# The modulation of a transformer block in units of 256 features, and two thirds of them later in the load order

## The chip, the cores and the metric

The kernel runs on one core of a Trainium2 chip. The metric is the device time of one execution in microseconds. PE is TensorE, DVE is VectorE, ACT is ScalarE, POOL is GpSimd and SP is SyncE, whose queue issues the weight loads.

## What is computed

The input is 256 tokens of 1024 features and one condition vector `c`. The first block modulates its layers by the condition, and only this block is touched:

```
cond = silu(c)                                   # 1024
mod  = cond @ ada_w + ada_b                      # 1024 x 6144
sh1, sc1, g1, sh2, sc2, g2 = split(mod, 6)       # 1024 features each
h = rms_norm(x, norm1) * (1 + sc1) + sh1
y = concat(attn_a(h), attn_b(h), gla(h), lru(h)) @ w_out     # each from its columns of h @ w_in
x = x + g1 * y
h = rms_norm(x, norm2) * (1 + sc2) + sh2
x = x + g2 * moe(h)                              # 32 experts, top 4
```

A second block of two layers with dense weights follows; it has no modulation.

## The kernel before

All is kept with features on the partitions. Weights come in units of 1 MB (128 x 2048 f32). `enqueue` lists the units of the first block in a fixed order, and `load` (line 306) issues the next load on SP's queue whenever one of five buffers is free: two of tag rawx, three of tag raw. A buffer is given back by `drop` (line 328), in the order of the program. There are two kinds of units.

A weight unit, of `w_in` (11 of them, the list WIN, line 1703: cqk, cv, cr, aq, ak, av, dx, dg, bq, bk, bv) or of `w_out` (wo1, four of them, in the order lru, attn_b, attn_a, gla), is split into two halves of 128 x 1024, each into a high part (a cast on ACT) and a low part (a subtraction on DVE or POOL). The raw buffer is free when its second low part is made. A product takes three matmuls (high x high, high x low, low x high), so a unit costs 48 matmuls of 256 columns (`unit_mm`, line 610; `vstep`, line 2263).

A modulation unit (`ada`, 24 of them) is used raw, by a function that stands in the queue beside it. In `ada_unit` (line 1758) the stationary operand is one eighth of `cond`, repeated to 32 columns, and the moving operand is the unit. Before, a unit holds 128 input rows of 2048 output features. Its four matmuls of 512 columns go to four strips of 32 partitions of one PSUM bank, and eight units, one per eighth of the input, add up there. After the eighth the bank is copied to SBUF, four transposes turn it and one DVE add with the bias fills 16 columns of `mod` (`ada_turn`, line 1780). Group 0 (units 0 to 7) gives sh1 and sc1, group 1 g1 and sh2, group 2 sc2 and g2. One bank is held from the first unit to the last.

`block1_units` (line 1692) sets the order of the loads: ada 0 to 7, cqk, cv, then each of the nine other weight units of `w_in` with two ada units behind it as far as these last, then the four of wo1.

The order of the instructions on each engine is made when the program is built. A planner (class Clocks, line 43) keeps a modelled clock of each engine and of the DMA. While the matmuls of a projection are written out, `stir` (line 485) steps other work between them: the four branches gla, aa (attn_a), ab (attn_b) and lru are generators, each started when its projections are there. Where a branch must be finished, `rounds` (line 502) steps what is ready first. Both call `pump` (line 356), which also makes the splits ahead and uses modulation units: a unit is used when the planner's clock of PE has come to within 0.5 us of its modelled landing. `use_up` forces all units up to a number. On the chip each engine works through its list in order; a modelled landing that comes later on the chip is a wait of the whole engine.

In `mixer1` (line 2271) the mean square and the eight normed rows z come first. Then `use_up(7)` forces the first eight modulation units, A = (1 + sc1) * norm1 is made in one instruction, and a loop over the eight feature tiles k makes the modulated rows (ACT Identity with scale and bias, two DVE operations for the low part). cqk and cv are split at k = 0 and k = 3, and from k = 3 on their products, and those of the small weight for gla, follow feature by feature. Then come the nine projections. `use_up` of unit 23 stands ahead of the products with wo1; ahead of the last of them (gla's) `settle` finishes all deferred small work. The experts' weights go to tiles of the next phase, in the memory of the mixer's pages.

Of the kernel before, what the change touches and what calls it, by code (L numbers as in the profile page):

```python
# [14 lines left out]
ALU = mybir.AluOpType  # L15
P = 128
T = 256
KD = 8
# [177 lines left out]
class Core:  # L196
    EARLY, SOON, MORE, POOL, ACT, PLAIN, LEAN = 0.7, 0.0, 2.0, 2.0, 1.0, -2.0, 0.5
    static = False
    FINE, LATE = 2, 1.0
    stepping = GIVE = False  # L200
    KEEP = ("raw", "whi", "wlo", "ident", "causal", "ones_d", "ones_g", "eps", "one", "one32", "junk", "id16", "s5_r4", "vecs")
    MID = ("iota", "four", "group", "upper", "ones", "mod", "adaA", "rw", "rb")
    NRAW = 3
# [2 lines left out]
    pages, stop = None, 1 << 30  # L206
# [149 lines left out]
    def pump(self):  # L356

        c = self.nc
        while self.sl < self.sh and c.written(self.halves[self.sl][0]) <= max(c.tensor.clock, min(self.v.clock, self.q.clock)) + self.SOON:
            self.split_low()  # L360
        while self.sh <= min(self.most, 2 * self.last - 1) and self.arrived(self.order[self.sh // 2], c.scalar) and self.free(c.scalar):
            self.split_high()
        for u in sorted(self.uses):
            if not self.arrived(u, c.tensor):
                break
            self.use(u)

# [1312 lines left out]
class Kernel(Block2):  # L1680
    NE, B1, NP42, NP22, NP12, NPAIR = 32, 2.0, 9, 8, 10, 4
    MIX = dict(EARLY=0.2, SOON=-0.5, LEAN=2.0, GIVE=True)
    WAT = 0, 3
    S3 = 0
    DM3 = 6
    DM1, DM2 = 7, 7
# [5 lines left out]
    def block1_units(self):  # L1692
        a = self.a
        ada = [(("ada", u), a["adaw"][u], lambda raw, n, u=u: self.ada_unit(u, raw, n)) for u in range(24)]
        win = [((n, 0), a["win1"][i]) for n, i in self.WIN]
        yield from ada[:8] + win[:2]
        for j, u in enumerate(win[2:]):
            yield u
            yield from ada[8 + 2 * j:10 + 2 * j]
        for g in self.YORD:  # L1700
            yield ("wo1", g), a["wo1"][g]

    WIN = [("cqk", 6), ("cv", 7), ("cr", 8), ("aq", 0), ("ak", 1), ("av", 2), ("dx", 9), ("dg", 10), ("bq", 3), ("bk", 4), ("bv", 5)]
    YORD = (3, 1, 0, 2)
# [47 lines left out]
    def ada_load(self):  # L1752
        c8, self.cond = self.t([P, KD], "c8"), self.t([P, KD, 32], "cond")
        self.nc.scalar.dma_start(c8, self.a["c"])
        self.nc.scalar.activation(self.cond, c8[:, :, None].to_broadcast([P, KD, 32]), AF.Silu)
        self.mod = self.t([P, 48], "mod")

    def ada_unit(self, u, raw, n):

        nc = self.nc  # L1760
        g, k = divmod(u, KD)
        if not u:
            self.adaps = self.bank()
        lab, self.lab = self.lab, "ada"
        for i in range(4):
            nc.tensor.matmul(self.adaps[i * 32:i * 32 + 32], self.cond[:, k], raw[:, i * 512:i * 512 + 512], start=k == 0, stop=k == KD - 1,
                             skip_group_check=True, tile_position=(0, i * 32))
        if k == KD - 1:
            rows = self.t([P, 512], "adarow")
            nc.scalar.copy(rows, self.adaps)  # L1770
            if g == 2:
                self.give(ps=1)
            if g:
                self.defer(lambda: self.ada_turn(g, rows))
            else:
                for _ in self.ada_turn(g, rows):
                    pass
        self.lab = lab

    def ada_turn(self, g, rows):  # L1780

        nc = self.nc
        yield from self.need(ps=1)
        self.lab = "ada"
        ps = self.psum()
        for j in range(4):
            nc.tensor.transpose(ps[:, j * P:(j + 1) * P], rows[:, j * P:(j + 1) * P], self.ident)
        yield
        at = lambda t: t[:, g * 16:g * 16 + 16].rearrange("p (i j) -> p i j", j=4)
        self.v.tensor_tensor(at(self.mod), ps.rearrange("p (j i r) -> p i j r", j=4, r=32)[:, :, :, 0], at(self.vec("adab")), op=ALU.add)  # L1790
        self.give(ps=1)

    def ada_norm(self, x, ms, g, sh, sc, emit):
        v = self.v
# [476 lines left out]
    def mixer1(self, x):  # L2271
        nc, a = self.nc, self.a
        v, q = self.v, self.q
# [13 lines left out]
            sq = self.square(x[:, 2 * i:2 * i + 2].rearrange("p a t -> p (a t)"), sq)  # L2287
        ms = self.mean([sq], self.ones_d)
        z = self.unit_rows(x, ms)
        self.use_up(7)  # L2290
        xn = self.fm(dt=F32R), self.fm(dt=F32R)
        A = self.t([P, KD], "adaA", 2)
        v.scalar_tensor_tensor(A, self.mod[:, 8:16], 1.0, self.vec("norm1"), op0=ALU.add, op1=ALU.mult)
        gps, pss = self.bank()[:16, :T], [self.bank() for _ in range(2)]
        ws, done = [], 0
        for k in range(KD):
            if k in self.WAT:
                j = len(ws) // 2
                self.split_ahead(2 * j + 1, v)
                ws += [self.half((self.WIN[j][0], 0), 2 * j + 1 + i) for i in range(2)]  # L2300
            t, sc, sh = self.p1(), A[:, k:k + 1], self.mod[:, k:k + 1]
            nc.scalar.activation(xn[0][k], z[k], AF.Identity, scale=sc, bias=sh)
            v.tensor_scalar(t, z[k], sc, sh, op0=ALU.mult, op1=ALU.add)
            v.tensor_sub(xn[1][k], t, xn[0][k].bitcast(F32))
            if k == 1:
                self.split(gw, *gwh)
            while k > 2 and done <= k:
                j, done = done, done + 1
                xs = xn[0][j], xn[1][j]
                for m in range(2):  # L2310
                    self.mm3(pss[0][:, m * T:(m + 1) * T], [w[:, j * P:(j + 1) * P] for w in ws[m]], xs, j == 0 and m == 0, j == KD - 1)
                self.vstep(pss[1], ws[2 + j // 4], xs, j)
                self.mm3(gps, (gwh[0][:, j], gwh[1][:, j]), xs, j == 0, j == KD - 1)
        self.split_ahead(self.uh + self.S3)
        y = self.fm(dt=F32R), self.fm(dt=F32R)
# [21 lines left out]
        for j, (n, _) in enumerate(self.WIN):  # L2337
            self.lab = n
            ps = pss[j] if j < 2 else self.bank()
# [30 lines left out]
                    ths[i] = self.spawn(self.attn_a(b[:2], b[2], y) if i == 0 else self.attn_b(b[:2], b[2], y) if i == 1 else  # L2370
                                        self.gla(*b, gl, wg2, rg, y) if i == 2 else self.lru(*b, y))
        acc = None
        self.use_up(self.keys.index(("ada", 23)))
        for g in self.YORD:
            self.finish(ths[g])
            acc = acc or [self.bank() for _ in range(4)]
            self.lab = "wo1"
            first, last = g == self.YORD[0], g == self.YORD[-1]

            def part(i, m, w):  # L2380
                self.mm3(acc[m // 2][:, (m % 2) * T:(m % 2 + 1) * T], [z[:, m * P:(m + 1) * P] for z in w],
                         (y[0][2 * g + i], y[1][2 * g + i]), first and i == 0 and m % 2 == 0, last and i == 1)
            if last:
                self.settle()
                ws = [self.half(("wo1", g), i + 1) for i in range(2)]
                for b in range(4):
                    for i in range(2):
                        for m in (2 * b, 2 * b + 1):
                            part(i, m, ws[i])
                sqs = []  # L2390

                def add(i):
                    v.tensor_add(sqs[i][:, :T], sqs[i][:, :T], sqs[i][:, T:])
                    if i:
                        v.tensor_add(sqs[i][:, :T], sqs[i][:, :T], sqs[i - 1][:, :T])
                for i in range(4):
                    for k in (2 * i, 2 * i + 1):
                        v.scalar_tensor_tensor(x[:, k], acc[i][:, (k % 2) * T:(k % 2 + 1) * T], self.mod[:, 16 + k:17 + k], x[:, k],
                                               op0=ALU.mult, op1=ALU.add)
                    sqs.append(self.p2([P, 512]))  # L2400
                    nc.scalar.activation(sqs[i], x[:, 2 * i:2 * i + 2].rearrange("p a t -> p (a t)"), AF.Square)
                    if i:
                        add(i - 1)
                break
            for i in range(2):
                w = self.half(("wo1", g))
                for m in range(KD):
                    part(i, m, w)
                    if m % self.FINE == self.FINE - 1 and m < KD - 1:
                        self.stir(self.budget)  # L2410
                self.tick(self.budget)
# [534 lines left out]
def host_block1(d, vecs, off):  # L2946
    c = np.ascontiguousarray
    f = lambda n: np.asarray(d[n])[0]
    out = {}
# [4 lines left out]
        vecs.append(v.reshape(-1, P).T)  # L2954
    out["x"] = c(np.asarray(d["x"])[0].T.reshape(8, P, T).transpose(1, 0, 2))
    out["c"] = c(np.asarray(d["c"]).reshape(8, P).T)
    out["adaw"] = c(f("ada_w").reshape(8, P, 3, 2048).transpose(2, 0, 1, 3).reshape(24, P, 2048))
    addv("adab", f("ada_b"))
    addv("norm1", f("norm1_g"))
    addv("norm2", f("norm2_g"))  # L2960
    w = f("w_in")
    sizes = (256, 256, 256, 256, 256, 256, 128, 128, 256, 16, 256, 256, 256)
    p = dict(zip("aq ak av bq bk bv cq ck cv cg cr dx dg".split(), np.split(w, np.cumsum(sizes)[:-1], axis=1)))
# [77 lines left out]
```

## Time and profile before

| | us |
|---|---|
| median of 3 runs | 2945.7 |
| lowest and highest | 2922.97, 2946.81 |
| the profiled execution | 2948.41 |
| its span, first to last instruction | 2946.7 |
| PE busy in it | 2673.1 (91%) |
| DVE, ACT, POOL busy | 1670.8, 1009.0, 423.4 |
| mean granted clock of PE | 0.967 |

The durations in the rows below are of the one profiled execution. Nearly all instructions are recorded by one helper, so they all carry line 172; they are told apart by the names of their tiles, which begin with the part of the program that made them. The units' buffers are called raw and rawx, high and low parts whi and wlo, and the first letters of a buffer's name are those of the part that happened to issue its load. The granted clock is 1.00 at 2.4 GHz and 0.50 at 1.2 GHz; a value between them is a mean over the stretch.

### The profile page before, as it was taken

Reading aid. Unit: us, or ns where it says so; the run is one execution under the profiler, and the core shown is the slowest. Engines: PE = TensorE matmul, PEld = TensorE weight load, DVE = VectorE, ACT = ScalarE, POOL = GpSimd, SP = SyncE. Lnnn points to the kernel's source line nnn. Section 1 sums busy time; section 2 is a strip of 40 time slices with the busy share of each in tenths; the row PEclk is TensorE's granted clock in tenths of the full one; section 3 lists DMA queues with packets and bytes.
Section 4 is the critical chain, followed back from the end, with each engine's and each line's share of the span. In section 5 each row is a group of like instructions: output and inputs, shape, how many; then the busy total and the mean of one; then the engine's idle time right before and its main releaser. Section 6 shows DMA issues by size and latency. Waiting matters only on the chain.

```text
span 2946.7 us, 55258 instructions
## 1 busy us (share of the span) xinstructions
PE 2673.1 (91%) x22931; PEld 2049.9 (70%) x22931; DVE 1670.8 (57%) x2968; ACT 1009.0 (34%) x1474; POOL 423.4 (14%) x386
## 2 busy tenths in 40 slices
PE   6867898988898888988999999889999999998998
PEld 3656333332333333368999999889999999998998
DVE  3485324242333311056679787667575698977755
ACT  3273100001000000033454655434454455654544
POOL 2322100000000000034012131143010100221100
PEclk7788999999999999999999999999999999999999
DMA  8504999999999999977554544377455455553453
GB/s 333 214 31 146 420 420 405 415 420 420 420 415 416 420 419 419 418 243 206 203 184 167 189 172 170 137 160 241 172 189 180 149 180 189 186 190 125 159 185 115
DMA packets 145421, 754.62 MB, mean 256 GB/s; under 512 B 45760, under 2 KB 50320, under 8 KB 58640
## 3 DMA queue, kind: packets, MB, share of 16 engines
q1 hardware_dynamic: 127584, 710.42, 63.2%
q0 software_dynamic: 17440, 40.61, 5.3%
q8 instruction: 185, 3.03, 0.4%
q14 instruction: 68, 0.56, 0.1%
q10 hardware_dynamic: 144, 0.00, 0.0%
HBM read 735.98 MB, written 14.97 MB: 255 GB/s over the span
## 4 chain that ended last, share of the span: by engine, by line
PE 45%; DVE 7%; DMA 2%; ACT 2%; issue 1%; ACTq 0%; DVEq 0%
PE ffn_ps L172 21%; PE x_ps L172 4%; PE bb_ps L172 3%; PE z_ps L172 3%; PE glu_ps L172 3%; PE g_ps L172 3%; PE bnd_ps L172 2%; PE wo_ps L172 2%; DMA ffn_raw<-gu 1%; DVE ffn_wlo L172 1%; PE ssd_ps L172 1%; PE u_ps L172 1%; DVE ffn_p L172 1%; DVE x_p L172 1%; DVE bnd_p L172 1%
## 5 line engine op out<-in xcount | busy, mean ns | idle before, releaser
L172 PE MATMUL ffn_ps<-bnd_p,ffn_whi 128*128 128x256 f32 x2560 | 468.3, 285 | 0.5 <-ACT ffn_whi L172 0.5
L172 DVE TENSOR_TENSOR ffn_wlo<-ffn_raw,ffn_whi 128x1024 fp32r<-128x1024 f32 x232 | 305.5, 1322 | 189.9 <-ACT ffn_whi L172 189.8
L172 PEld LDWEIGHTS ffn_ps<-bnd_p,ffn_whi 128*128 128x128 f32 x2560 | 404.0, 194 | 0.9 <-ACT ffn_whi L172 0.9
L172 PE MATMUL ffn_ps<-bnd_p,ffn_wlo 128*128 128x256 f32 x1280 | 365.7, 286 | 17.5 <-DVE ffn_wlo L172 17.5
L172 ACT CAST ffn_whi<-ffn_raw 128x1024 fp32r<-128x1024 f32 x232 | 240.6, 1046 | 310.8 <-PE ffn_ps L172 242.1
L172 PE MATMUL down_ps<-up_place,tr_p 128*32 128x512 f32 (+1 forms) x2048 | 243.1, 612 | 81.1 <-DMA up_place<-edn 81.1
L172 PE MATMUL ffn_ps<-ffn_p,ffn_whi 128*128 128x256 f32 x1408 | 259.6, 286 | 11.3 <-ACT ffn_whi L172 11.3
L172 PEld LDWEIGHTS ffn_ps<-bnd_p,ffn_wlo 128*128 128x128 f32 x1280 | 248.5, 194 | 19.0 <-DVE ffn_wlo L172 19.0
L172 PE MATMUL up_ps<-down_place,prep_p 128*32 128x512 f32 (+1 forms) x1920 | 224.7, 596 | 21.0 <-DMA down_place<-eup 21.0
L172 PE MATMUL up_ps<-up_place,prep_p 128*32 128x512 f32 (+1 forms) x2048 | 230.5, 595 | 7.5 <-DMA up_place<-eup 7.0
L172 PEld LDWEIGHTS down_ps<-up_place,tr_p 128*32 128x32 f32 x2048 | 68.2, 112 | 243.0 <-issue 202.9
L172 PEld LDWEIGHTS ffn_ps<-ffn_p,ffn_whi 128*128 128x128 f32 x1408 | 223.3, 195 | 11.7 <-ACT ffn_whi L172 11.7
L172 DVE TENSOR_SCALAR glu_p<-up_ps 128x512 f32<-128x512 f32 x64 | 44.2, 691 | 311.2 <-PE up_ps L172 311.2
L172 PE MATMUL ffn_ps<-ffn_p,ffn_wlo 128*128 128x256 f32 x704 | 201.5, 286 | 1.1 <-DVE ffn_wlo L172 1.1
L172 PEld LDWEIGHTS up_ps<-up_place,prep_p 128*32 128x32 f32 x2048 | 61.8, 109 | 149.8 <-issue 129.8
L172 PEld LDWEIGHTS up_ps<-down_place,prep_p 128*32 128x32 f32 x1920 | 57.0, 109 | 130.7 <-issue 127.0
L172 DVE COPY scat_p<-down_ps 128x512 f32<-128x512 f32 x16 | 11.1, 692 | 240.4 <-PE down_ps L172 240.4
L172 PEld LDWEIGHTS ffn_ps<-ffn_p,ffn_wlo 128*128 128x128 f32 x704 | 137.1, 195 | 1.9 <-DVE ffn_wlo L172 1.9
L172 DVE TENSOR_TENSOR ffn_p<-ffn_p,ffn_p 128x256 f32<-128x256 f32 (+1 forms) x184 | 99.6, 547 | 41.6 <-ACT ffn_p L172 41.4
L172 ACT COPY prep_p<-prep_ps 128x512 f32<-128x512 f32 x16 | 9.4, 585 | 291.2 <-PE prep_ps L172 291.2
L172 ACT COPY tr_p<-tr_ps 128x512 f32<-128x512 f32 x32 | 18.7, 585 | 223.6 <-PE tr_ps L172 223.6
L172 PE MATMUL bb_ps<-ssd_p,ba_whi 128*128 128x256 f32 x416 | 84.2, 302 | 9.5 <-ACT ssd_p L172 6.1
(794 smaller groups left out, 5887.4 us busy)
## 6 DMA issues: line engine op xcount, KB each, us to landing
up_place<-eup SPq DMA_DIRECT2D x128, 1024.0 KB, 10.8
up_place<-edn SPq DMA_DIRECT2D x128, 1024.0 KB, 13.7
down_place<-eup SPq DMA_DIRECT2D x120, 1024.0 KB, 14.7
ffn_raw<-gu SPq DMA_DIRECT2D x75, 1024.0 KB, 4.9
ffn_raw<-dn SPq DMA_DIRECT2D x40, 1024.0 KB, 5.0
x_raw<-win SPq DMA_DIRECT2D x22, 1024.0 KB, 5.0
z_raw<-win SPq DMA_DIRECT2D x16, 1024.0 KB, 5.1
g_raw<-win SPq DMA_DIRECT2D x10, 1024.0 KB, 4.9
```

The lines of the kernel that those rows point to most:

```text
L172: return f(out, *args, **kw)
```

## The change

A modulation unit now holds all 1024 input rows of 256 output features, and is complete by itself. The host sorts the features so that unit k of the first eight has features 128k to 128k+127 of sh1 and of sc1; units 8 to 23 take the other 4096 in order. A unit is eight matmuls of 256 columns, two into each strip of 32 partitions; a copy of 128 x 256 on ACT, two small matmuls with a constant matrix `four`, which add up the four strips and turn the result, and one DVE add of two columns. `mixer1` forces unit k only at feature tile k, and makes A there, column by column.

The load order becomes: ada 0, 1, cqk, ada 2, 3, cv, ada 4 to 7, cr, aq, ak, then av, dx, dg, bq, bk and bv with one ada unit behind each (8 to 13), wo1 of lru, ada 14 to 17, wo1 of attn_b, ada 18 to 23, wo1 of attn_a, wo1 of gla. `pump` uses a unit only when the planner's clock of PE is 2 us past its modelled landing, and a PSUM bank and one of two places for modulation units are free. `use_up` of unit 23 moves to just ahead of the last product with wo1.

```diff
@@ Core
+    ADAM, PSADA = 2.0, 0
@@ pump
         for u in sorted(self.uses):
-            if not self.arrived(u, c.tensor):
+            if u not in self.raws or c.written(self.raws[u][0]) > c.tensor.clock - self.ADAM or not self.has(dict(ps=1 + self.PSADA, ada=1)):
                 break
             self.use(u)
@@ Kernel
+    ADA0, ADA1, ADAM = 5, (4, 6, 0, 0), 2.0
@@ block1_units
-        yield from ada[:8] + win[:2]
-        for j, u in enumerate(win[2:]):
+        yield from ada[:2] + win[:1] + ada[2:4] + win[1:2] + ada[4:8]
+        rest = iter(ada[8:])
+        for j, u in list(enumerate(win))[2:]:
             yield u
-            yield from ada[8 + 2 * j:10 + 2 * j]
-        for g in self.YORD:
+            if j >= self.ADA0:
+                yield next(rest)
+        for g, n in zip(self.YORD, self.ADA1):
             yield ("wo1", g), a["wo1"][g]
+            for _ in range(n):
+                yield next(rest)
@@ ada_unit, ada_turn (new)
+        self.grab(ps=1, ada=1)
+        ps, w = self.psum(), raw.rearrange("p (k c) -> p k c", k=KD)
+        for k in range(KD):
+            i = k % 4
+            nc.tensor.matmul(ps[i * 32:i * 32 + 32, :T], self.cond[:, k], w[:, k], start=k < 4, stop=k >= 4, skip_group_check=True,
+                             tile_position=(0, i * 32))
+        if u < 8:
+            for _ in self.ada_turn(u, ps):
+                pass
+        else:
+            self.defer(lambda: self.ada_turn(u, ps), after=ps[:, :T])
...
+        rows = self.t([P, T], "adarow", 2)
+        nc.scalar.copy(rows, ps[:, :T])
         yield
+        for j in range(2):
+            nc.tensor.matmul(ps[:, T + j * 32:T + j * 32 + 32], rows[:, j * P:(j + 1) * P], self.four, start=True, stop=True, skip_group_check=True)
+        yield
+        at = self.ada_at(u)
+        self.v.tensor_tensor(self.mod[:, at], ps[:, T:T + 64].rearrange("p (j r) -> p j r", r=32)[:, :, 0], self.vec("adab")[:, at], op=ALU.add)
+        self.give(ps=1, ada=1)
@@ mixer1
-        self.use_up(7)
...
-        v.scalar_tensor_tensor(A, self.mod[:, 8:16], 1.0, self.vec("norm1"), op0=ALU.add, op1=ALU.mult)
...
+            self.use_up(self.keys.index(("ada", k)))
+            v.scalar_tensor_tensor(A[:, k:k + 1], self.mod[:, 8 + k:9 + k], 1.0, self.vec("norm1")[:, k:k + 1], op0=ALU.add, op1=ALU.mult)
...
-        self.use_up(self.keys.index(("ada", 23)))
         for g in self.YORD:
...
             if last:
+                self.use_up(self.keys.index(("ada", 23)))
                 self.settle()
```

## Rows read from the trace of the kernel before

**Rows 1.** The table by stage: busy us and instructions of each engine, granted clock, DMA.

```profile
core 0: us, PE busy (x) PEld busy (x) DVE busy (x) ACT busy (x) POOL busy (x), PEclk, DMA share, GB/s
...
60.30:136.70 76.40, 61.73 (x372) 45.59 (x368) 33.05 (x57) 19.79 (x31) 22.41 (x14) 0.75 0.66 248
136.70:179.30 42.60, 42.60 (x395) 38.62 (x394) 34.32 (x57) 24.51 (x41) 20.36 (x10) 1.00 0.30 104
179.30:217.90 38.60, 14.82 (x73) 10.51 (x72) 29.15 (x78) 31.25 (x93) 5.52 (x3) 0.74 0.00 1
217.90:249.40 31.50, 28.93 (x221) 27.86 (x222) 15.86 (x31) 12.25 (x23) 12.52 (x5) 0.88 0.00 1
...
290.00:1250.00 960.00, 848.20 (x7418) 317.86 (x7414) 284.52 (x829) 71.69 (x125) 25.60 (x39) 0.99 1.01 417
```

**Rows 2.** The timeline of SP's DMA queue: start us, us, what.

```profile
17.29 3.60 SPq L172 DMA_DIRECT2D mix_raw<-win  x2
...
254.13 23.37 SPq L172 DMA_DIRECT2D moe_place<-eup  x8
```

**Rows 3.** The list of PE's waits, 60.3 to 179.3 us.

```profile
PE mix_ps L172 <- DMA aq_raw<-adaw: 7.7, 2, 4.9
PE mix_ps L172 <- DMA cr_raw<-adaw: 5.1, 4, 1.7
PE gla_ps L172 <- DVE gla_p L172: 1.7, 1, 1.7
```

**Rows 4.** The timeline of PE, three stretches: start us, us, what, [wait].

```profile
14.22 1.03 PE L172 MATMUL mix_ps<-k_raw,k_cond 128*32 128x512 f32 x8
...
81.33 1.07 PE L172 MATMUL mix_ps<-cr_raw,k_cond 128*32 128x512 f32 x8 [1.74 <-DMA cr_raw<-adaw]
...
93.05 1.94 PE L172 MATMUL mix_ps<-aq_raw,k_cond 128*32 128x512 f32 x8 [2.84 <-DMA aq_raw<-adaw]
...
95.72 0.63 PE L172 MATMUL aq_ps<-mix_p,cr_whi 128*128 128x256 f32 x2
96.15 0.41 PE L172 MATMUL aq_ps<-mix_p,cr_wlo 128*128 128x256 f32 x1
...
140.17 0.39 PE L172 MATMUL dx_ps<-mix_p,ak_whi 128*128 128x256 f32 x2
140.40 0.28 PE L172 MATMUL dx_ps<-mix_p,ak_wlo 128*128 128x256 f32 x1
```

**Rows 5.** The same, only gla_ps: PE, PEld, DVE, ACT, clock, DMA share, GB/s.

```profile
60.30:136.70 76.40, 12.64 (x82) 10.62 (x82) 7.36 (x11) 0.00 (x0) 0.75 0.66 248
```

**Rows 6.** The same, only k_cond: PE, PEld, ACT, clock, DMA share, GB/s.

```profile
11.30:28.80 17.50, 11.80 (x64) 1.76 (x64) 0.00 (x0) 0.76 1.02 421
...
60.40:179.40 119.00, 15.57 (x97) 2.18 (x96) 0.00 (x0) 0.84 0.53 196
```

**Rows 7.** The timeline of all engines where the first modulation is finished.

```profile
13.38 2.50 DVE L172 TENSOR_TENSOR mix_p<-k_h,mix_p 128x512 f32<-128x512 f32 x4
...
29.25 2.00 ACT L172 CAST mix_whi<-mix_raw 128x1024 fp32r<-128x1024 f32 x2
...
30.62 0.17 DVE L172 TENSOR_TENSOR k_mod<-ada_ps,k_vecs 128x16 f32<-128x16 f32 x1 [14.73 <-PE ada_ps L172]
...
30.91 2.36 DVE L172 TENSOR_TENSOR mix_wlo<-mix_raw,mix_whi 128x1024 fp32r<-128x1024 f32 x2
...
33.62 1.09 ACT L172 ACTIVATE mix_p<-mix_p,k_mod,mix_adaA 128x256 fp32r<-128x256 f32 x2
...
34.27 1.04 PE L172 MATMUL mix_ps<-mix_p,mix_whi 128*128 128x256 f32 x2 [3.70 <-ACT mix_p L172]
```

**Rows 8.** DMA issues of the first 300 us: count, KB, median us to landing.

```profile
aq_raw<-win SPq DMA_DIRECT2D x3, 1024.0 KB, 4.9
```

**Rows 9.** The timeline of ScalarE, a copy of this size from PSUM.

```profile
232.18 0.37 ACT L172 CAST mix_p<-ab_ps 128x256 fp32r<-128x256 f32 x1 [0.22 <-PE ab_ps L172]
```

**Rows 10.** The timeline of PE, two small matmuls.

```profile
261.29 0.31 PE L172 MATMUL moe_ps<-k_ident,route_p 32*128 32x32 f32 x2 [0.56 <-ACT route_p L172]
```

More of the change, by code (lines that the diff above doesn't have):

```diff
@@ L1756, in ada_load, with ada_at @@
         self.mod = self.t([P, 48], "mod")
+        self.room["ada"] = 2
+    def ada_at(self, u):
+        return slice(u, u + 9, 8) if u < 8 else slice(2 * u, 2 * u + 2)
     def ada_unit(self, u, raw, n):
         nc = self.nc
-        g, k = divmod(u, KD)
-        if not u:
-            self.adaps = self.bank()
+        self.grab(ps=1, ada=1)
         lab, self.lab = self.lab, "ada"
-        for i in range(4):
-            nc.tensor.matmul(self.adaps[i * 32:i * 32 + 32], self.cond[:, k], raw[:, i * 512:i * 512 + 512], start=k == 0, stop=k == KD - 1,
-                             skip_group_check=True, tile_position=(0, i * 32))
@@ L1768, in ada_unit @@
[L1768 to L1777, printed above, removed]
+        ps, w = self.psum(), raw.rearrange("p (k c) -> p k c", k=KD)
[3 more added lines that the diff above has]
+                             tile_position=(0, i * 32))
@@ L1778, in ada_unit, with ada_turn @@
+        if u < 8:
[3 more added lines that the diff above has]
+            self.defer(lambda: self.ada_turn(u, ps), after=ps[:, :T])
         self.lab = lab
-    def ada_turn(self, g, rows):
+    def ada_turn(self, u, ps):
         nc = self.nc
[L1783 to L1787, printed above, removed]
-        yield
-        at = lambda t: t[:, g * 16:g * 16 + 16].rearrange("p (i j) -> p i j", j=4)
-        self.v.tensor_tensor(at(self.mod), ps.rearrange("p (j i r) -> p i j r", j=4, r=32)[:, :, :, 0], at(self.vec("adab")), op=ALU.add)
-        self.give(ps=1)
+        rows = self.t([P, T], "adarow", 2)
+        nc.scalar.copy(rows, ps[:, :T])
+        yield
+        for j in range(2):
[4 more added lines that the diff above has]
+        self.give(ps=1, ada=1)
@@ L2956, in host_block1 @@
     out["c"] = c(np.asarray(d["c"]).reshape(8, P).T)
-    out["adaw"] = c(f("ada_w").reshape(8, P, 3, 2048).transpose(2, 0, 1, 3).reshape(24, P, 2048))
+    order = np.concatenate([np.arange(16).reshape(2, 8).T.reshape(-1), np.arange(16, 48)])
+    out["adaw"] = c(f("ada_w").reshape(8, P, 48, P)[:, :, order].reshape(8, P, 24, 2 * P).transpose(2, 1, 0, 3).reshape(24, P, 2048))
     addv("adab", f("ada_b"))
```

## The prediction

> **What bounds the kernel now.** Read first the table by stage [rows 1]; its borders are where cr's products begin (60.3), where av's end (136.7), where the last projection ends (179.3), where the first product with wo1 starts (217.9) and where the last ends (249.4). From 290 to 1250 us the 16 DMA engines are full (share 1.01, 417 GB/s): the experts are bound by their weights. Their first load is issued at 254.13, just behind the mixer [rows 2], because its buffers lie in the mixer's pages. So whatever the mixer gains or loses moves all the rest by the same amount, and only the first 250 us are in question.
>
> In those, the stretch 60.3 to 136.7 stands out: four projections (cr, aq, ak, av) in 76.4 us, at a mean granted clock of 0.75, while the next 42.6 us hold five at clock 1.00. The list of PE's waits says why: 7.7 + 5.1 = 12.8 us are waits for DMA of modulation units (aq_raw and cr_raw from adaw) and 1.7 us for VectorE [rows 3]. PE works in order, so a projection whose weights are long there stands behind a modulation unit that is still being loaded. The timeline of PE shows the second price: behind a wait of 2.84 us the unit took 1.94 us where another took 1.07, and the products that followed ran 0.215 us apart where those at 140 us ran 0.115 apart (two in 0.43 against 0.23) [rows 4]. That is 1.2 against 2.4 GHz.
>
> The stage splits so. 192 products (4 x 48) at 0.114 us are 21.8 us. The products of gla were busy 12.64 us [rows 5]; times the clock of 0.75, 9.5 us at full clock. The 12 modulation units after 60.4 were busy 15.57 us [rows 6]; 11 of them lie before 136.7, about 14.5 us with 0.8 for their four transposes 15.3. Waits are 14.5. The rest of 76.4, 15.3 us, is what the half clock cost.
>
> Behind 179.3 PE works 14.82 of 38.6 us while ScalarE is busy 31.25 and VectorE 29.15 [rows 1]. That is a chain of softmax and norms, not of loads.
>
> **The change, part by part.**
>
> *The lead (to the first product of cr, now 60.3).* Now eight units come first, at 421 GB/s or 2.49 us each [rows 6], then cqk and cv; the modulation is complete at 31 us and products start at 34.27 [rows 7]. After: ada0, ada1, cqk, ada2, ada3 fill the five buffers at once; cqk is third and lands near 13.8, as the third unit does now (PE takes it at 14.22 [rows 4]). Its two casts (2.00 us) and two subtractions (2.36 us) stand behind the four products of unit_rows on VectorE, which end at 15.9 [rows 7], so its buffer is free at 18.3. Only then can SP issue cv, and ada4 to ada7 are queued behind it although their buffers are free earlier; now the same queue issues win units at 17.29 [rows 2]. With 4.9 us from issue to landing [rows 8] cv lands at 23.2 and ada4 to ada7 at 25.7, 28.2, 30.7, 33.2. cv's split then lets products start at about 27.5, 7 us earlier than now. Features 0 to 3 are 60 products: taking half of them at 0.215 us and half at 0.114, since the clock starts low there, they end at 37.3. From there each feature is a round of its own, in order on PE: the unit 1.07 us, a copy of 128x256 on ScalarE 0.37, two small reducing matmuls near 0.31 [rows 9, 10], two VectorE steps of 0.17, one ScalarE Identity of about 0.5 [rows 7], with some 0.6 us of hand-overs, then 15 products, 1.7 us. That is 4.9 us, four rounds 19.6, end 57. PE would be busy only about two thirds of a round, so I add 3 us for a fallen clock: 60. Now four more units (24 less the 8 and 12 of rows 6) stand between the lead's products and cr, and hold PE until 60.3; these go. Lead: 0, bounds -4 and +10.
>
> *cr to av.* The modulation units leave this stretch, and the loads that PE waited for with them. A weight unit takes 2.49 us to load and 5.5 us to multiply, so loads are no bound. Left are 21.8 + 9.5 = 31.3 us. I add 3 us for the clock to come back after the lead and 3 for waits on VectorE, whose 33 us of work in this stretch [rows 1] no longer find the pauses they had: 37, against 76.4, so -39. Bounds: 31 with neither, 55 if the half clock still costs its 15 and VectorE 8.
>
> *dx to bv.* Here stood one unit and four transposes, 1.7 us. Now some seven of the 16 late units (six lie between the weights, the seventh to ninth behind bv are loaded while it runs) at 1.07 + 0.31 us = 9.6. Work of gla that cr to av had time for comes here, about 3 us of PE, and VectorE is busy 34.3 of 42.6 us already, so 4.5 us more of waits: 42.6 - 1.7 + 9.6 + 3 + 4.5 = 58, +15. Bounds +5 (units in gaps, no waits) and +23.
>
> *The tail, 70.1 us.* Nine units remain. Their matmuls, 12 us, fit into the 23.8 us that PE idles between 179.3 and 217.9. Nine copies of 0.37 us go in front of others on ScalarE, 3.3 us, most of them in its pauses; nine adds of 0.17 us on VectorE. A unit is placed only when the planner's clock is 2 us past its modelled landing, so no new DMA wait is expected. +2, bounds -4 (matmuls in the gap hold up the clock, now 0.74) and +12 (each unit between two links of the chain).
>
> Over all, 24 copies take the place of three larger ones, 24 adds that of three, 48 reducing matmuls that of 12 transposes; these are in the sums above. Sum: 0 - 39 + 15 + 2 = -22 us. The profiled execution took 2948.4 us (span 2946.7), so it would be 2926.4; the median of the runs shown is 2.7 lower, 2945.7, which gives **2923.7 us**.
>
> [...] Behind the wait of 2.84 us matmuls ran at the lower clock, behind one of 1.74 us they did not [rows 4]. [...]
>
> **The rivals.**
>
> A. *The rounds of the lead run at half clock.* Unit 1.94, products 3.2, the rest unchanged: 7.3 us a round, 9.6 in all instead of the 3 I allow, and cr to av starts slow too, 3 us: -22 + 10 = -12, 2934. For it: 0.75 in rows 1. Against it: PE is denser than in the waits that cost the clock. Chance 0.10.
>
> B. *VectorE becomes the bound.* It did 33 us in the 76.4 us of cr to av. In 37 us it may do 22; the other 11 land behind, where it is busy 34.3 of 42.6 and 29.2 of 38.6, and become about 14 us of time at that use. Gain 8, 2938. Against it: while it waits for PE today, it would not. Chance 0.15.
>
> C. *Nothing is given back.* cr to av 32, dx to bv +8, tail -3: -44 + 8 - 3 = -39, 2907. For it: 137 to 179 at clock 1.00 with no wait although VectorE is as busy as that. Chance 0.22.
>
> D. *Slower: the late units are not taken in the tail.* A unit now needs a free PSUM bank beside the landing. If aa, ab and lru hold the banks, the units are only taken when use_up forces them before the last product with wo1. Then the loads of up to ten units and of wo0 and wo2 behind them follow one another: 12 x 2.49 + 4.9 = 35 us, and 4 to 5 for the last chain. -22 + 40 = +18, 2964. At about 4 us a unit it decides from six units left on. Against it: the one bank that the modulation held throughout is free now, and PE idles there. Chance 0.06.
>
> My forecast has 0.47, with a range of its own of 2912 to 2936.
>
> **How the numbers follow.** One per cent, 29 us, is about what a measurement of this kernel can tell from no change (its three runs lie 24 us apart). Faster by more than that, below 2916: C, 0.22, and the fast end of the forecast, 0.10, together 0.32. Slower by more than that, above 2975: D at its worst with the lead's bound, 0.05. The rest, 0.63. The range runs from 2900 (most of C) to 2946: it takes in A and B and leaves out D and the two ends, about 0.16.
>
> **What would show it.** Right: no PE wait for adaw between 60 and 180; cr to av in about 37 us at a clock near 1; bv ends near 155; the first expert load near 232. For the lead: cr's first product between 56 and 64, and between rounds PE waits of near 2 us for ScalarE and VectorE. Wrong: cr starting near 70 (A); VectorE over 90% busy from 100 to 200 and the tail longer by over 10 us (B); a run of adaw loads right before the last product with wo1, or PE waiting there (D); the mixer ending earlier but the expert loads not (then the chain behind it is not what I take it for).

## The result and the profile after

The changed kernel takes 2964.98 us (median of 9, 2957.39 to 2977.73) against 2941.56 (median of 9) for the kernel before beside it: ratio 1.0077, 95% interval 1.0056 to 1.0099. It is 0.8% slower; the forecast was 22 us less. The profiled execution took 2968.99 us, span 2967.3 [before: 2946.7].

The first expert load moved by 19.1 us, the span by 20.6, and the experts' stage runs as before [rows 1, 2]: the loss lies in the first mixer. The timeline of SP's queue after:

```profile
273.19 23.54 SPq L172 DMA_DIRECT2D moe_place<-eup  x8
```

The table by stage after, cut where cr's products begin, where av's end, where the last projection ends and where the last product with wo1 ends, and the experts:

```profile
core 0: us, PE busy (x) PEld busy (x) DVE busy (x) ACT busy (x) POOL busy (x), PEclk, DMA share, GB/s
70.20:103.90 33.70, 31.94 (x292) 27.89 (x290) 25.24 (x32) 21.22 (x32) 17.76 (x9) 1.00 0.72 274
103.90:197.50 93.60, 76.80 (x603) 62.80 (x601) 42.69 (x94) 33.03 (x68) 29.73 (x24) 0.76 0.48 174
197.50:268.40 70.90, 54.29 (x380) 46.32 (x379) 44.75 (x105) 41.49 (x106) 14.24 (x7) 0.76 0.00 1
...
310.00:1270.00 960.00, 847.48 (x7394) 317.26 (x7390) 284.56 (x829) 71.77 (x125) 25.63 (x39) 0.99 1.01 416
```

| stage | before | forecast | after |
|---|---|---|---|
| to cr's first product | 60.3 | 60 | 70.2 |
| cr to av | 76.4 | 37 | 33.7 |
| dx to the last projection | 42.6 | 58 | 93.6 |
| tail, to the end of wo1's products | 70.1 | 72 | 70.9 |

cr to av gave what was forecast. dx to bv took it all back, and 8 us more. PE's waits from cr to bv (reader, releaser, total, times, longest), against [rows 3]:

```profile
PE ada_ps L172 <- DMA dx_raw<-adaw: 8.6, 3, 3.4
PE ada_ps L172 <- ACT ada_adarow L172: 4.5, 3, 3.5
PE ada_ps L172 <- DMA bk_raw<-adaw: 4.1, 1, 4.1
PE gla_ps L172 <- DVE gla_p L172: 0.7, 1, 0.7
PE ada_ps L172 <- DMA bq_rawx<-adaw: 0.6, 1, 0.6
```

The waits for adaw are back at another place: 13.3 us where there were 12.8. The timelines of PE and of SP's queue show how one looks (a unit's eight matmuls are 16 records):

```profile
130.84 1.46 PE L172 MATMUL ada_ps<-dx_raw,k_cond 128*32 128x256 f32 x16 [3.36 <-DMA dx_raw<-adaw]
137.26 1.94 PE L172 MATMUL ada_ps<-dx_raw,k_cond 128*32 128x256 f32 x16 [2.69 <-DMA dx_raw<-adaw]
144.20 1.94 PE L172 MATMUL ada_ps<-dx_raw,k_cond 128*32 128x256 f32 x16 [2.57 <-DMA dx_raw<-adaw]
```

```profile
113.75 0.33 SPq L172 DMA_DIRECT2D dx_raw<-wo  x1
117.18 22.40 SPq L172 DMA_DIRECT2D dx_raw<-adaw  x4
146.19 0.33 SPq L172 DMA_DIRECT2D dx_raw<-wo  x1
```

Four units are issued over 22.4 us, each when the one before has been multiplied: bq, bk, bv and wo1 of lru hold the other four buffers, and one buffer goes round, issue, landing, matmuls, next issue, 6 to 9 us each time. PE stands before each of the three units shown, and the second and third take 1.94 us for 1.07, as in [rows 4]. The units' busy time (eight matmuls and nothing else) by stage, against [rows 6], columns PE, PEld, ACT:

```profile
70.20:103.90 33.70, 4.28 (x64) 1.67 (x64) 0.00 (x0) 1.00 0.72 274
103.90:197.50 93.60, 18.19 (x192) 6.70 (x192) 0.00 (x0) 0.76 0.48 174
```

So four late units stand before dx, twelve between dx and bv, and none in the tail, where nine were forecast.

The other loss is in the lead. It has two parts. The first is the start of the products. A line of SP's queue, and the one wait of PE in the products of features 0 to 3:

```profile
22.36 0.33 SPq L172 DMA_DIRECT2D mix_raw<-win  x1
```

```profile
33.82 0.58 PE L172 MATMUL mix_ps<-mix_wlo,mix_p 128*128 128x256 f32 x1 [2.01 <-DVE mix_wlo L172]
```

The load at 22.36 is cv's. The second part is the four rounds of features 4 to 7. One of them in PE's timeline (its last line is cut by the window), and the table by stage of the first round, cut where its products begin:

```profile
49.65 1.07 PE L172 MATMUL ada_ps<-mix_rawx,k_cond 128*32 128x256 f32 x16
51.27 0.63 PE L172 MATMUL ada_ps<-k_four,ada_adarow 128*128 128x32 f32 x4 [0.55 <-ACT ada_adarow L172]
53.05 1.04 PE L172 MATMUL mix_ps<-mix_p,mix_whi 128*128 128x256 f32 x2 [1.15 <-ACT mix_p L172]
53.89 0.42 PE L172 MATMUL mix_ps<-mix_p,mix_wlo 128*128 128x256 f32 x1
54.10 0.63 PE L172 MATMUL mix_ps<-mix_p,mix_whi 128*128 128x256 f32 x2
...
56.60 0.64 PE L172 MATMUL ada_ps<-mix_raw,k_cond 128*32 128x256 f32 x8
```

```profile
42.60:46.00 3.40, 1.70 (x21) 0.94 (x21) 0.76 (x4) 0.97 (x2) 0.00 (x0) 1.00 0.34 80
46.00:49.60 3.60, 3.60 (x15) 2.99 (x15) 0.41 (x1) 0.00 (x0) 0.00 (x0) 0.53 0.52 216
```

Unit 1.07, wait 0.55, reduction 0.63, wait 1.15, 15 products in 3.6: 7 us a round, and the products at half clock behind 3.4 us in which PE worked 1.70.

### The profile page after: what moved, and what is told of

Same layout as the page of the kernel before. It is cut to its first block, busy times and chain, and to the rows that moved or that the text cites. A ratio compares the mean times of both kernels' runs of the same rounds, so it can differ in the third digit from the quotient of the medians.

```text
span 2967.3 us, 55904 instructions
## 1 busy us (share of the span) xinstructions
PE 2697.7 (91%) x23207; PEld 2076.1 (70%) x23207; DVE 1674.3 (56%) x2990; ACT 1016.0 (34%) x1495; POOL 418.6 (14%) x392
## 4 chain that ended last, share of the span: by engine, by line
PE 43%; DVE 7%; DMA 3%; ACT 2%; issue 1%; POOL 0%; ACTq 0%; DVEq 0%
PE ffn_ps L172 19%; PE x_ps L172 4%; PE bb_ps L172 3%; PE z_ps L172 3%; PE glu_ps L172 3%; PE g_ps L172 3%; PE bnd_ps L172 2%; DMA ffn_raw<-gu 2%; PE wo_ps L172 2%; DVE ffn_wlo L172 1%; PE ssd_ps L172 1%; DMA ffn_raw<-dn 1%; DVE ffn_p L172 1%; DVE bnd_p L172 1%; PE u_ps L172 1%
## 5 line engine op out<-in xcount | busy, mean ns | idle before, releaser
L172 DVE COPY scat_p<-down_ps 128x512 f32<-128x512 f32 x16 | 11.1, 692 | 246.0 <-PE down_ps L172 246.0
```

The costliest lines, as they stand in the source:

```text
L172: return f(out, *args, **kw)
```

## The experiments

Three theories. **T1**: the planner prices a unit wrongly. It charges PE `free_size * 0.0017` for each f32 matmul, 3.5 us for a unit's eight; the chip takes 1.07 (at full clock). Every unit sets the planner's clock of PE 2.4 us further ahead of the chip, and a margin of 2 us behind a modelled landing is used up by one. (The kernel before had a margin too: `MIX` sets SOON to -0.5 in this mixer, so a unit was used when the planner's clock was 0.5 us past the modelled landing, and not already up to 0.5 us ahead of it.) **T2**: units take single PSUM banks that the blocks of gla and aa wait for. **T3**: the lead's rounds, whose steps follow one another, cost its 10 us. "First load" below is the issue of the first expert load; behind it the profiled executions took 2680 to 2703 us, so differences of a few us are read from the first load and not from one span.

**The right charge**

```diff
@@ on_tensor
         x = args[1]
+        if args[0].free_size() == 32 and x.free_size() == T and x.dtype != F32R:
+            return 0.13
```

> The changed kernel, with one thing different: the planner charges a unit matmul (32 rows wide in, 256 columns out) 0.13 us, which is what eight in 1.07 us take in the changed kernel's lead, where it charged about 0.44 (eight of them 3.5 us). So its TensorE clock no longer runs ahead of the chip, and units are placed later: by its order two to six in each of bq, bk and bv where the changed kernel had all sixteen before bv. T1 (units placed before their features have landed, one load buffer going round): TensorE's waits for adaw between dx's first product and bv's last fall from 13.3 us (8.6 dx, 4.1 bk, 0.6 bq) to under 4, the granted clock of the stretch rises from 0.76 to 0.88 or more, the stretch falls from 93.6 us to 65-75, the first expert load comes at 245-258 in place of 273.2, and the time falls by 15 to 28 us, to 2937-2950. T2 (units take the banks for which gla and aa wait): the same units still take single banks, the stretch and the tail together stay within 5 us of 164.5 and so does the time. T3 (the lead) expects no change of the lead: cr's first product at 70.

Measured: ratio 0.9928 (0.9895 to 0.9962), 2925.3 us; first load 234.04. Its table by stage (67.7 cr, 96.2 dx, 168.3 last projection) and PE's waits from cr to bv:

```profile
67.70:96.20 28.50, 28.50 (x256) 25.82 (x255) 17.89 (x26) 20.23 (x29) 11.98 (x7) 1.00 0.69 256
96.20:168.30 72.10, 66.68 (x634) 53.02 (x632) 56.52 (x107) 38.51 (x80) 35.34 (x26) 0.95 0.67 253
168.30:229.30 61.00, 51.39 (x385) 43.99 (x383) 44.26 (x99) 36.82 (x97) 13.68 (x7) 0.83 0.00 1
```

```profile
PE ada_ps L174 <- ACT ada_adarow L174: 2.8, 1, 2.8
PE gla_ps L174 <- POOL gla_p L174: 1.7, 1, 1.7
PE gla_ps L174 <- DVE gla_p L174: 0.9, 3, 0.3
```

Not one wait for adaw is left from cr to bv, although thirteen late units now stand in dx to bv in place of twelve, and the granted clock is 0.95 for 0.76. That is T1's sign; the gain was larger than it expected, 39 us of first load, and how much of it is the waits and how much the new order is settled by the run without the waits, below. cr starts 2.5 us sooner, which no theory had. The condition also matches the router's eight matmuls, but these come behind the first load. The time is that of the blind forecast (0.9925), with one constant more, but by other stages (28.5, 72.1 and 61.0 us where it had 37, 58 and 72), so the agreement is partly luck.

**A wider margin**

```diff
-    ADA0, ADA1, ADAM = 5, (4, 6, 0, 0), 2.0
+    ADA0, ADA1, ADAM = 5, (4, 6, 0, 0), 7.0
```

> The changed kernel, with the margin behind a modelled landing 7 us in place of 2, charges as they were. T1: the waits for adaw from dx to bv fall from 13.3 us to under 5; but the units still bunch in bq and bk, where the planner's clock is furthest ahead, so the stretch falls only to 75-85 us; the first expert load at 258-266, the time 7 to 15 us under the changed kernel's 2965. T2: banks are taken as before, within 5 us of 2965. Lead: no change, cr's first product at 70.

Measured: ratio 0.9956 (0.9929 to 0.9983); waits for adaw 3.0 us, first load 239.89. The stretch is as T1 expected (78.6 us), but the gain in time, ratio 1.0077 to 0.9956 or some 35 us, is over twice what it expected. Of 33 us of first load 15 came from the stretch, 15 from the tail and 5 from the lead; the last two are an effect of the order that T1 had not.

**The same order without the waits**

```diff
@@ ada_unit
-        ps, w = self.psum(), raw.rearrange("p (k c) -> p k c", k=KD)
+        ps, w = self.psum(), raw.rearrange("p (k c) -> p k c", k=KD) if u < 8 else self.xin
...
+        nc.mark(raw, nc.tensor.clock)
```

> The changed kernel with TensorE's order unchanged to the last matmul (the same places, the same banks, the same charges), but the sixteen late units multiply x, which is resident, in place of their features, which are still loaded. This leaves the last two thirds of the modulation uncomputed (values of x stand for them); it takes the waits for their loads away and nothing else from TensorE. T1 (the waits for adaw, 13.3 us, and the half clock that follows them): dx to bv falls from 93.6 us to 60-72 at a clock of 0.88 or more, the first expert load from 273 to 235-252, time 2928-2945. T2 (the order itself: units ahead of the blocks of gla and aa, and single banks): only the 13 us go, dx to bv 78-84 us, first expert load 257-262, time 2948-2955.

Measured: first load 250.43. Only the part up to there can be read: the modulation has other values, and the run takes 7408 us, presumably because the experts' routing takes another path. Its table by stage:

```profile
68.10:101.80 33.70, 31.94 (x292) 27.85 (x290) 25.32 (x33) 21.22 (x32) 17.74 (x9) 1.00 0.82 306
101.80:175.10 73.30, 66.66 (x602) 56.50 (x600) 42.96 (x94) 33.10 (x68) 30.01 (x24) 0.88 0.55 207
175.10:245.70 70.60, 50.95 (x379) 44.54 (x379) 45.36 (x105) 41.40 (x106) 14.67 (x7) 0.81 0.00 1
```

With the order held to the last matmul, the waits and what followed them cost 20.3 us of dx to bv (93.6 to 73.3). That lies in neither range, nearer to T1's 60 to 72 than to T2's 78 to 84; the clock (0.88) and the first load are T1's. PE's 76.80 busy us became 66.66 for the same instructions: 10 of the 20 were clock, the rest idle time. Against the right charge 16 us are still missing: 9.6 in the tail and 5.2 in cr to av, by the rows of both. So about half of what the right charge gains is the waits, shown with the order held; the other half is the order that the charge makes, and which places in it make the tail longer was not settled.

**One more buffer; the charge doubled**

```diff
-            with k.phase(2, 4, 12, 15, 30, n1):
+            with k.phase(3, 4, 12, 12, 30, n1):
```

> The changed kernel with one more 8 KB buffer for raw weights (three of the second kind in place of two; three fewer half-size buffers for the mixers), charges as they were. With it the planner sees loads land earlier in its own time and places all sixteen units before bq. If the single buffer that goes round is the cause by itself (rival): the waits for adaw from cr to bv fall under 5 us, and the time under 2945. If the cause is the planner's clock that runs ahead (T1): units are again placed before they have landed, waits for adaw of 8 us or more, now from av to dg, clock of that stretch under 0.85, and the time not under 2945, though the tail may be shorter by some us, since bq and bk are free of units.

Measured: ratio 1.0128 (1.0087 to 1.0169), first load 303.51. The single buffer is no cause by itself: with a sixth buffer (and three fewer of the mixers' small ones) the planner places units earlier still, nine in cr to av where there were four, and the waits for adaw grow to 32.5 us:

```profile
PE ada_ps L172 <- DMA dx_raw<-adaw: 16.7, 5, 5.1
PE ada_ps L172 <- DMA av_raw<-adaw: 11.4, 4, 5.0
...
PE ada_ps L172 <- DMA aq_rawx<-adaw: 4.4, 2, 3.1
```

```diff
-            return 0.13
+            return 0.87
```

> The changed kernel with the charge doubled in place of cut: 0.87 us for a unit matmul, 7 us a unit. The planner then does all eight first units ahead of the 120 products, as in the run with the old lead (cr's first product at 61-65), and places all sixteen late units before bq. T1: they stand there long before they land; waits for adaw of 15 us or more from av to dg, granted clock of that stretch under 0.80, cr to the last bv in the row 140-165 us, the time 2965-2995 in spite of the better lead. T2 or no effect of the charge: waits for adaw of 10 us or less, time 2935-2955 (the changed kernel with the old lead had 2945).

Measured: ratio 1.0099 (1.0066 to 1.0132), 2976.7 us, first load 286.07, waits for adaw 26.3 us; cr to the last projection 149.1 us, at 0.81 to av's end and 0.70 behind:

```profile
64.10:116.90 52.80, 42.83 (x334) 36.12 (x331) 17.60 (x32) 21.52 (x32) 25.14 (x16) 0.81 0.61 220
116.90:213.20 96.30, 76.72 (x557) 61.98 (x555) 47.92 (x109) 35.69 (x82) 25.64 (x17) 0.70 0.41 145
```

So the first load follows the charge: 234.0 at 0.13 us a matmul, 273.2 at 0.44, 286.1 at 0.87, the last in spite of a lead 6 us shorter.

**The kernel before with the right charge**

```diff
@@ on_tensor
         x = args[1]
+        if args[0].free_size() == 32 and x.free_size() == 512 and x.dtype != F32R:
+            return 0.27
```

> The kernel before, unchanged but for the planner's charge for a unit's matmul (0.27 us for 512 columns, four in 1.07 us, where it charged 0.87). If the charge was the cause of the waits in cr to av already: TensorE's waits for adaw there fall from 12.8 us to under 4, cr to av from 76.4 us to 45-55, dx to bv rises from 42.6 to 50-60 since more units fall there, the first expert load comes at 236-246 in place of 254, ratio 0.992-0.997: most of what the changed form gains with a right charge needs no new form. If it is the new form (units complete by themselves, single banks, a margin of 2 us) that lets them be placed well: the waits stay above 8 us, first expert load 250-256, ratio 0.998-1.002.

Measured: ratio 0.9923 (0.9893 to 0.9954), first load 226.57, no wait for adaw at all from cr on. Its table by stage (55.6 cr, 95.1 end of av, 156.4 last projection):

```profile
55.60:95.10 39.50, 37.56 (x307) 29.60 (x303) 31.05 (x47) 19.41 (x29) 12.17 (x8) 1.00 0.95 372
95.10:156.40 61.30, 56.76 (x466) 46.04 (x466) 43.43 (x73) 26.88 (x45) 26.75 (x15) 0.92 0.49 174
156.40:221.80 65.40, 42.31 (x293) 36.98 (x293) 44.56 (x108) 43.57 (x115) 14.47 (x6) 0.82 0.00 1
```

The charge was the cause already, and more of one than that expectation held. cr to av goes from 76.4 us to 39.5 with the loads in the old order, two units behind each weight unit, and the DMA engines busy 0.95 of the time; 19 of these 37 us come back in dx to bv (61.3 for 42.6). What that stretch suffered from was not the place of the loads but that of the units: with the old charge (3.5 us for a unit of 1.07, there too) they stood ahead of their landing. The change moved units away from the waits and kept what made them.

**The old load order with the right charge**

```diff
-            if j >= self.ADA0:
-                yield next(rest)
+            if j < 10:
+                yield next(rest)
+                yield next(rest)
...
-    ADA0, ADA1, ADAM = 5, (4, 6, 0, 0), 2.0
+    ADA0, ADA1, ADAM = 5, (0, 0, 0, 0), 2.0
```

> The charge of 0.13 us, but the spread undone: two units are loaded behind each weight unit from cr on, as in the kernel before; no unit is late. It tells what the spreading itself brings, once the placing is right. If the spread pays as forecast (39 us back in cr..av, 15 spent in dx..bv): cr to av takes 45-60 us, dx to bv 50-60, the first expert load comes 8 to 20 us behind the 234.0 of the charge alone, ratio 0.996-1.000. If it was only the placing that cost, and the order of loads is indifferent (rival): first expert load within 4 us of 234, ratio within 0.9915-0.9945.

Measured: ratio 0.9955 (0.9933 to 0.9977), first load 243.23. cr to av took 35.7 us, less than expected, without a DMA wait at 343 GB/s; dx to bv 67.0, more than expected, tail 66.3. With the units' new form the spreading is worth 9 us of first load (243.2 to 234.0), the low end of its theory: it gives 7 us in cr to av and 5 in the tail and costs 5 in dx to bv; the other 2 lie in the lead. The intervals of the two ratios, this one and 0.9928, overlap, so the 9 us rest on one profiled execution each.

**The lead**

```diff
-            while k > 2 and done <= k:
+            while k > 2 and done <= (k if k == KD - 1 else k - 1):
```

> The changed kernel with one thing different in the lead: the products of feature j stand behind the modulation of feature j+1, so that TensorE has 15 products to do while ScalarE and VectorE make the next feature. Nothing else in the order moves. T3 (a round in series: unit, copy, reduction, mix, products, 6.95 us each, of which 1.7 us are TensorE's waits for ScalarE): the rounds fall to 4.5-5.3 us, cr's first product comes at 60-64 in place of 70.2, and the first expert load and the time move down by 6 to 10 us. Against it: if the lead is paced by the arrival of the units' features, or if the clock stays at half in it, cr starts at 68-70 and the time is within 3 us of 2965. T1 and T2: the stretch from dx to bv stays at 93 us within 5.

Measured: ratio 1.0020 (0.9993 to 1.0048); cr's first product at 58.41, first load 262.39, 10.8 us earlier; dx to bv unchanged. T3 holds. The round is now 3.98 us, at full clock throughout:

```profile
46.43 0.63 PE L172 MATMUL ada_ps<-k_four,ada_adarow 128*128 128x32 f32 x4 [0.55 <-ACT ada_adarow L172]
46.89 0.48 PE L172 MATMUL mix_ps<-mix_p,mix_whi 128*128 128x256 f32 x2
47.21 0.28 PE L172 MATMUL mix_ps<-mix_p,mix_wlo 128*128 128x256 f32 x1
...
48.79 1.07 PE L172 MATMUL ada_ps<-mix_raw,k_cond 128*32 128x256 f32 x16
50.41 0.63 PE L172 MATMUL ada_ps<-k_four,ada_adarow 128*128 128x32 f32 x4 [0.55 <-ACT ada_adarow L172]
```

```diff
-        yield from ada[:2] + win[:1] + ada[2:4] + win[1:2] + ada[4:8]
+        yield from ada[:8] + win[:2]
...
+        self.use_up(7)
...
-            self.use_up(self.keys.index(("ada", k)))
```

> The changed kernel with the lead of the kernel before in the new form: all eight first units are loaded ahead of cqk and cv and done before the first modulation, and the 120 products of cqk and cv then stand in a row as in the kernel before. The late units stay spread. T3: cr's first product comes back to 59-62 (60.3 before), the first expert load and the time are 8 to 11 us under the changed kernel's; T1 and T2: dx to bv stays at 85-95 us, so the time is still within 12 us of the kernel before and not under it by more than 5.

Measured: ratio 0.9996 (0.9959 to 1.0033), cr's first product at 63.51, first load 256.77. The lead gained less than expected (6.7 us); the rest of the 16 us of first load is the balance of the stages behind it, where the planner now put the late units elsewhere: waits for adaw 10.4 us, dx to the last projection 76 us, not the 85 to 95 of the expectation. Any edit ahead of the late units reshuffles them, which is why the order-preserving run above was needed.

**Banks**

```diff
-    ADAM, PSADA = 2.0, 0
+    ADAM, PSADA = 2.0, 3
```

> The changed kernel, but a unit is placed only while four banks of PSUM are free in place of one, so the blocks of gla and aa are not kept from theirs; charges as they were. T2: gla's and aa's blocks move forward, VectorE is busier from dx to bv (42.7 of 93.6 us in the changed kernel, over half then), and the tail of 70.9 us falls by 10 or more, time 2935-2955. T1: the charge is as wrong as before, waits for adaw stay at 8 us or more; what changes is only by units that slip behind bq, time 2945-2970, the tail within 6 us of 70.9.

Measured: ratio 0.9985 (0.9962 to 1.0009), first load 252.32, tail 63.5, VectorE 56.8 of 80.0 us from dx to bv. That is most of what T2 expected (the time, 2943.9, in its range; the tail 7.4 us shorter, not 10), but the waits for adaw fell to 1.4 us, which T1 had not expected and which T2 doesn't need: asking for more banks also makes units late, so this run alone decides nothing. With the right charge beside it (both edits as above):

> The charge of 0.13 us and four free banks for a unit: by the order eight of the sixteen late units now stand behind bv among the last blocks of gla, aa and lru, where the prediction had nine. T2 (units keep gla and aa from banks): 5 us or more under the charge alone, ratio 0.990 or lower. T1 (banks don't matter once the waits are gone): dx to bv shorter by about eight units (8 to 12 us), the tail longer by what these cost there, the sum within 4 us, ratio 0.9915-0.9945. The prediction's own term of 2 us for nine units in the tail holds if the tail (63 us with the charge alone) grows by under 4 us beyond the blocks that move with it, and falls if it grows by 8 or more.

Measured: ratio 0.9918 (0.9891 to 0.9945), as with the charge alone (0.9928); first load 228.89. dx to bv 61.0 us (11.1 less), tail 69.9 (8.9 more):

```profile
93.30:154.30 61.00, 54.28 (x462) 47.47 (x460) 52.31 (x93) 33.96 (x67) 30.31 (x19) 0.91 0.53 194
154.30:224.20 69.90, 61.55 (x556) 49.23 (x556) 50.11 (x119) 41.08 (x111) 15.08 (x9) 0.91 0.25 91
```

The two stages together are 2.2 us shorter, inside T1's 4; of the 5.2 us of first load the rest lies before dx, 2.4 of it in the lead. So T2 is not borne out as a cause of its own; a few us of it are not excluded. Eight units now stand in the tail, and it grew by 8.9 us: my 2 us for nine fall too, as far as the blocks of gla and aa that moved with them don't explain the 8.9.

**Both edits that helped** (the charge of 0.13, and the products one feature behind)

> The changed kernel with both edits: the planner charges 0.13 us for a unit matmul, and the lead's products of feature j stand behind the modulation of feature j+1. If the two losses lie one after the other (the lead ends before dx begins): cr's first product at 58-61, from there to the last bv in the row 98-102 us as with the charge alone (67.8 to 166), the first expert load at 224-228, and a ratio to the kernel before of 0.988-0.990 (0.9928 less about 9 of 2945 us). If the edits share their gain (what starts sooner then waits for its loads, DMA share above 0.75 from cr on): ratio 0.991-0.994, with TensorE's waits for adaw or win above 4 us from cr to bv.

Measured: ratio 0.9872 (0.9839 to 0.9904), 2909.5 us, the fastest of all; first load 224.61:

```profile
56.10:89.20 33.10, 33.10 (x307) 29.41 (x305) 22.88 (x34) 21.34 (x32) 12.91 (x8) 1.00 0.68 257
89.20:158.20 69.00, 64.42 (x603) 52.42 (x602) 54.22 (x110) 37.75 (x85) 32.16 (x20) 0.95 0.68 247
158.20:219.90 61.70, 44.52 (x364) 39.52 (x364) 38.47 (x93) 33.88 (x89) 10.77 (x5) 0.83 0.00 1
```

The two losses add: 9.4 us of first load beyond the charge alone, as the first expectation had it. Two variants of it, the first:

```diff
-    ADAM, PSADA = 2.0, 0
+    ADAM, PSADA = 2.0, 3
```

> Both edits of the fastest so far (charge 0.13, products one feature behind) and four free banks for a unit, as a candidate. T2: under 0.9850. T1: within 0.9855-0.9890, since the five units that move behind bv cost there what they cost before.

The second:

```diff
-    ADA0, ADA1, ADAM = 5, (4, 6, 0, 0), 2.0
+    ADA0, ADA1, ADAM = 3, (4, 4, 0, 0), 2.0
```

> Both edits, and the late units loaded earlier: one behind each weight unit from aq on (eight), four behind the gate of lru and four behind the next, in place of six, four and six. If loads are not what bounds cr to bv any more: TensorE's busy time there stays, ratio 0.985-0.989. If a unit ahead of a weight load still delays it: waits for win of 3 us or more between cr and dx, and ratio 0.990 or more.

Measured: 0.9922 (0.9896 to 0.9948) and 0.9934 (0.9910 to 0.9958), first loads 227.78 and 233.81; neither is better. Both ratios lie above what was expected of an indifferent order, and the second has no wait for win, so the reason given for that case fails too. What made both slower than 0.9872 is open: each has one long wait of PE for VectorE in ab (9.0 and 10.8 us), but the run before them has one too (11.7).

## Why the prediction was wrong, step by step

**What bounds the kernel.** Right: all behind the first load moved by what the mixer lost (19.1 of the span's 20.6 us). The waits for adaw in the kernel before and the half clock behind them were read rightly too. What was not asked is why a unit stood there before it had landed. The answer was in the code shown: a charge of 3.5 us beside rows of 1.07.

**dx to bv: the step that failed.** "+15. Bounds +5 (units in gaps, no waits) and +23", and with it the sentence "A unit is placed only when the planner's clock is 2 us past its modelled landing, so no new DMA wait is expected". It was +51. What failed is that sentence: the margin is kept on the planner's clock, and that clock ran 2.4 us further ahead of the chip with each unit, so the units were placed before they had landed. The work was nearly sized right: 76.8 busy us at a mean clock of 0.76 are some 58 us at full clock (an estimate), where the forecast had 53.5 without its 4.5 of waits; with twelve units in place of seven, at its own 1.38 us each, it would have been 60. What came on top is 13.3 us of waits for adaw, 3.5 for ScalarE, and near 18 of half clock. Taking the waits alone away gives back 20.3 us, the right charge 39 over all stages.

**The lead: the second miss, at its bound.** Forecast 0, bounds -4 and +10; measured +9.9. Products began at 29.70 for 27.5, and features 0 to 3 ended at 42.6 for 37.3: 5 us. cv's load was issued at 22.36, where the sum has 18.3, and PE then stood 2.01 us for a low half. With the margin of 7 us cv was issued at 18.13 and the rounds began at 36.4; with the right charge, at 22.40 and 39.1. So part of the 5 us goes with that load; what held it, and the rest, were not followed up. The rounds took 27.6 us where 19.6 and 3 had been allowed: the other 5. The term missed in them is the 15 products, 3.6 us for 1.7: rival A, given 0.10, came true in the products (it had 3.2, and 7.3 a round), and "cr starting near 70" was its sign. The units themselves stayed at 1.07, which A had at 1.94, and cr to av did not start slow, which A had too (its clock is 1.00).

The Trainium skill, TensorE: Matmul & The Clock Gate, section HAM oscillation, tells of a loop of short matmul bursts with long waits for DMA between them, in which every burst starts throttled. The trace agrees in dx to bv, where behind waits of 2.69 and 2.57 us for adaw the units took 1.94 us for 1.07. The lead is another case, which that section does not tell of: its waits are 0.55 and 1.15 us, both for ScalarE, and the products of the first round still ran at 0.53. With the longer of the two filled by earlier products the clock stayed at 1.00.

**cr to av**: -42.7 for -39. Right in size and in what happened (no wait for adaw, clock 1.00), though four late units still stood there. But moving the loads was not needed for it: the kernel before with the right charge comes to 39.5 us with its loads where they were.

**The tail**: +0.8 for +2, but by luck, with no unit in it. The nine were all taken before, and the run that did put eight there found it 8.9 us longer.

**The rivals.** D had the sign and, by chance, the time (2964 against 2965), but not the mechanism: its units came too late, these too early. B and C did not occur in the changed kernel.

**Not tried**: the kernel before and the changed one, both with the right charge, in one comparison. Their ratios, 0.9923 and 0.9928, come from two; the intervals overlap, and also that of the first with the 0.9872 of the fastest.

## What to carry to other kernels

Where an order is fixed by a planner, compare its charge with the trace for each kind of instruction that the change moves. Behind a wait for a load ask first who put the consumer there, and only then what delays the load. A change that moves work away from such waits should be measured beside the one constant that makes them: here the constant alone brought the forecast gain, with the change or without it. Where a chain of small steps makes an engine wait, put the previous step's bulk work between its links; here that gave 10.8 us.

## What was not expected of the hardware

Half clock followed gaps shorter than the 1.74 us behind which [rows 4] show full clock: in the lead PE idled 0.55 and 1.15 us in a stretch of 3.4, and the next 3.6 us ran at 0.53. With only the 0.55 us left in a round of 3.98, sixteen us of rounds ran at 1.00. No run here separates the length of the gaps from the work between them:

```profile
42.40:58.40 16.00, 14.32 (x139) 11.42 (x140) 5.86 (x17) 4.46 (x8) 0.00 (x0) 1.00 0.79 263
```
